# The second MLP matrix with VectorE and ScalarE in source order, and its first G on GpSimd's queue

## The chip, the core and the metric

The kernel runs on one core of one Trainium2 chip. The time is device microseconds (us) of one execution. Five engines work side by side, each through its own list of instructions: TensorE (PE, with PEld for its weight loads), VectorE (DVE), ScalarE (ACT), GpSimd (POOL) and SyncE (SP). DMA transfers are issued from SP's and POOL's lists and move data by themselves.

## The reference

One layer of a diffusion backbone on 512 tokens of width 2048. The part that matters here is the end of the layer, a squared-ReLU MLP with a hidden width of 8192:

```
def sqrelu_mlp(h, w1, w2):
    return jnp.square(jax.nn.relu(h @ w1)) @ w2

x = x + g2 * rms_norm(sqrelu_mlp(modulate(rms_norm(x, norm_g[i, 2]), sh2, sc2), w_mlp_in[i], w_mlp_out[i]), norm_g[i, 3])
```

Everything is float32. Ahead of the MLP stand the modulation vectors, a norm, a Fourier mixing and a projection.

## The kernel before

**Precision.** A float32 operand is split in two: ACT casts it to a rounded high half (`hi`), DVE subtracts that from the operand and gets the low half (`lo`). Three matmuls then make one product (`mm3`, L122): high by low, low by high, high by high. The first of them reads the low half of the weights, so PE can't start a product before that half is there.

**First matrix.** The hidden rows are made in 32 units of 256 (`unit`, `unit_plain`). `unit` is a Strassen-like scheme: seven products A11, S1, S3, S2, A12, A22, S4 of sums of blocks instead of eight, each 24 matmuls with 256 columns. The sums of the left operand are in `comb`. The last unit (31) is a plain one. Each unit's squared Relu G is stored to DRAM (`square_out`, the tensors `gd`).

**Second matrix.** `second(c, j)` is called for seven chunks `c` of 1024 hidden rows and two halves `j` of the output columns: 14 calls of seven products, 24 matmuls of 128x512 each. For a product DVE first adds blocks of the weights (L941, L946, L950, L954; two instructions of 128x1024 each, A11, A12 and S4 need none), then `split` makes `hi` and `lo` of both weight halves (L119 on ACT, L120 on DVE). `hi` and `lo` have three buffers each, a product needs two, so the second half's cast waits until PE has read the first half of the product before. A product's sums are copied out of PSUM by ACT (L928, two copies) when the next product has been traced (`settle`), and POOL adds them to DRAM.

**The left operands** of a chunk come from G: `g_chunk` loads two tiles of 1 MB, `left_in` makes the seven left operands, each with a cast (L902, ACT) and a low half (L903, DVE), four of them with an addition or subtraction on DVE ahead (L891, L894, L897, L900; each 128x1024). The table `NEXT` says behind which product of the chunk before they are traced. Chunk 0's are all made ahead of the first product, at a higher priority. `early` loads two more units of G and splits them for the last part of the kernel.

**What sets the order.** A scheduler with a model of time orders every engine's list; code in `tc.manual_schedule(engines=...)` keeps the order of the source on the engines named, `issue_after(x)` puts instructions behind x on x's engine. Before, all of this stage was left to the scheduler, but for S1 of the first call, which stands behind the cast of S1's left operand. `stream` takes weight buffers in turn, ten in all, and its loads stand on SP's list.

Of the kernel before, what the change touches and what calls it, by code (L numbers as in the profile page):

```python
# [58 lines left out]
def block_kernel(ctx: ExitStack, tc, xs, c_l, w_mod, b_col, g_col,  # L59
# [54 lines left out]
    def as32(ap):  # L114
        return ap.bitcast(F32)
# [533 lines left out]
    def act_relu2(u, srcs):  # L649

        r = tmp4([P, 2, 512])
        for j in range(2):
            nc.scalar.activation(out=r[:, j, :], in_=srcs[j], func=AF.Relu)
        square_out(u, r)
# [120 lines left out]
    def settle():  # L775
        while owed:
            owed.pop(0)()

    def unit(u):

        b11, b12, b22, b21 = (stream(w_in_s[u - UNIT0, b].rearrange("p k f -> p (k f)")) for b in range(4))

        x_, y_ = bank(), bank()
        a_, b_, c_, d_ = x_[:, T0], x_[:, T1], y_[:, T0], y_[:, T1]

        def product(s, src, ps, start):
            wh, wl = hi4([P, 1024]), lo4([P, 1024])
            split(wh, wl, src)
            for k in range(8):
                ks = slice(k * P, (k + 1) * P)  # L790
                lh, ll = left_of(s, k)
                nc.tensor.matmul(ps, lhsT=wh[:, ks], rhs=ll, start=start and k == 0, stop=False, skip_group_check=True)  # L792
                nc.tensor.matmul(ps, lhsT=wl[:, ks], rhs=lh, start=False, stop=False, skip_group_check=True)  # L793
                nc.tensor.matmul(ps, lhsT=wh[:, ks], rhs=lh, start=False, stop=k == 7, skip_group_check=True)  # L794

        product("A11", b11, a_, True)
        flip[0] ^= 1
        both = raw("raw" if flip[0] else "rawm")
        nc.vector.tensor_add(out=both, in0=b11, in1=b12)
        product("S1", both, d_, True)  # L800
        settle()
        sn, r = tmp4([P, 4, 256]), tmp4([P, 1024])
        nc.scalar.copy(out=sn[:, 0], in_=a_)
        nc.vector.tensor_add(out=b12, in0=b12, in1=b22)
        product("S3", b12, c_, False)
        nc.scalar.copy(out=sn[:, 2:4].rearrange("p a t -> p (a t)"), in_=y_)
        nc.vector.tensor_add(out=b11, in0=b12, in1=b11)
        product("S2", b11, b_, False)
        product("A12", b21, a_, False)
        nc.vector.tensor_add(out=b12, in0=b11, in1=b21)  # L810
        product("A22", b12, c_, False)
        nc.vector.tensor_sub(out=sn[:, 1], in0=sn[:, 0], in1=b_)
        nc.vector.tensor_add(out=sn[:, 2], in0=sn[:, 2], in1=sn[:, 3])
        nc.vector.tensor_add(out=r[:, 768:1024], in0=sn[:, 1], in1=sn[:, 2])
        product("S4", b22, d_, False)
        nc.scalar.activation(out=r[:, 0:256], in_=a_, func=AF.Relu)
        nc.scalar.activation(out=r[:, 768:1024], in_=r[:, 768:1024], func=AF.Relu, scale=-1.0)

        def rest():
            nc.vector.tensor_add(out=r[:, 256:768].rearrange("p (a t) -> p a t", a=2), in0=y_.rearrange("p (a t) -> p a t", a=2),  # L820
                                 in1=sn[:, 1].unsqueeze(1).to_broadcast([P, 2, 256]))
            nc.scalar.activation(out=r[:, 256:512], in_=r[:, 256:512], func=AF.Relu)
# [44 lines left out]
    def g4(shape, dt=F32):  # L867
        return buf("g4", shape, dt)
# [1 line left out]
    PRODUCTS = ("A11", "S1", "S3", "S2", "A12", "A22", "S4")  # L870
    pacc = {(s, j): dp.tile([P, 2, 512], F32, name=f"p{s}{j}") for s in PRODUCTS for j in range(2)}
    left = [{} for _ in range(CHUNKS)]
    first_cast = []
    raws = [{} for _ in range(CHUNKS + 1)]

    def g_chunk(c):
        gf = [buf("ga", [P, 4, 512]) for _ in range(2)]
        for j in range(2):
            nc.sync.dma_start(out=gf[j].rearrange("p u t -> p (u t)"), in_=gd[c][:, j].rearrange("p u t -> p (u t)"))
        raws[c]["g"] = gf  # L880

    def left_in(c, s):

        st = raws[c]
        gf = st["g"]
        a11, a21, a12, a22 = gf[0][:, :, T0], gf[0][:, :, T1], gf[1][:, :, T0], gf[1][:, :, T1]
        if s in ("A11", "A12", "A22"):
            src = {"A11": a11, "A12": a12, "A22": a22}[s]
        elif s == "S1":
            src = st["v"] = tmp4([P, 4, 256])  # L890
            nc.vector.tensor_sub(out=src, in0=a22, in1=a21)  # L891
        elif s == "S3":
            src = tmp4([P, 4, 256])
            nc.vector.tensor_sub(out=src, in0=a11, in1=a21)  # L894
        elif s == "S2":
            src = st["v"]
            nc.vector.tensor_add(out=src, in0=src, in1=a11)  # L897
        else:
            src = st["v"]
            nc.vector.tensor_sub(out=src, in0=src, in1=a12)  # L900
        t = buf("ga" if s == "A11" else "s1" if s == "S1" and c % 2 == 0 else "sb", [P, 2, 4, 256], F32R)
        cast = nc.scalar.copy(out=t[:, 0], in_=src)  # L902
        nc.vector.tensor_tensor(out=t[:, 1], in0=src, in1=as32(t[:, 0]), op=ALU.subtract)  # L903
        left[c][s] = t
        return cast

    def second(c, j):

        def load(b):
            return [stream(w_out_s[c, j, b, h].rearrange("p k n -> p (k n)")) for h in range(2)]  # L910

        def product(s, src):
            ps = [bank(), bank()]
            for h in range(2):
                wh, wl = hi4([P, 1024]), lo4([P, 1024])
                split(wh, wl, src[h])
                for k in range(2):
                    ks = slice(k * 512, (k + 1) * 512)
                    for i in range(2):
                        ts = slice(i * P, (i + 1) * P)  # L920
                        t = left[c][s]
                        mm3(ps[i], t[:, 0, 2 * h + k, ts], t[:, 1, 2 * h + k, ts], wh[:, ks], wl[:, ks], h + k == 0, h + k == 2)
            settle()

            def out():
                ev = g4([P, 2, 512])
                for i in range(2):
                    nc.scalar.copy(out=ev[:, i, :], in_=ps[i])  # L928
                if c:
                    nc.gpsimd.dma_start(out=pacc[s, j], in_=ev, accum_op=ALU.add)  # L930
                else:
                    nc.gpsimd.dma_start(out=pacc[s, j], in_=ev)
            owed.append(out)
            for f in THEN.get((c, j, s), ()):
                f()

        b11, b12 = load(0), load(1)
        product("A11", b11)
        both = [g4([P, 1024]) for _ in range(2)]
        for h in range(2):  # L940
            nc.vector.tensor_add(out=both[h], in0=b11[h], in1=b12[h])  # L941
        b22 = load(2)
        with tc.issue_after(first_cast[0]) if c + j == 0 else nullcontext():
            product("S1", both)
        for h in range(2):
            nc.vector.tensor_add(out=b12[h], in0=b12[h], in1=b22[h])  # L946
        product("S3", b12)
        b21 = load(3)
        for h in range(2):
            nc.vector.tensor_add(out=b11[h], in0=b12[h], in1=b11[h])  # L950
        product("S2", b11)
        product("A12", b21)
        for h in range(2):
# [25 lines left out]
            nc.vector.scalar_tensor_tensor(out=oacc[2 + i][:, right_c], in0=u2[:, h], scalar=-1.0, in1=p["S1"][:, h], op0=ALU.mult, op1=ALU.subtract)  # L979


    NEXT = {(0, "A12"): ("A11",), (0, "S4"): ("S1",), (1, "A11"): ("S3",), (1, "A12"): ("S2",), (1, "S4"): ("A12", "A22")}
    THEN = {}
    for c in range(CHUNKS - 1):
        THEN[c, 0, "S3"] = [lambda c=c: g_chunk(c + 1)]
        for (j, s), what in NEXT.items():
            THEN[c, j, s] = [lambda c=c, n=n: left_in(c + 1, n) for n in what]
        THEN[c + 1, 0, "S1"] = [lambda c=c: left_in(c + 1, "S4")]

    gts = {}  # L990

# [10 lines left out]
            g_in(u, lambda: (t[:, 0], t[:, 1]))  # L1002
        oacc.extend(buf("sb" if i else "ga", [P, D]) for i in range(4))

    THEN[CHUNKS - 1, 0, "A12"] = [early]
    with tc.high_priority(offset=AHEAD):
        g_chunk(0)
        for s in PRODUCTS:
            cast = left_in(0, s)
            if s == "S1":  # L1010
                first_cast.append(cast.ins)
            if s == "S3":
                with tc.issue_after(cast.ins):
                    act_relu2(UNITS - 1, last)
    for c in range(CHUNKS):
        for j in range(2):
            second(c, j)
    settle()

    f0, f1 = LAST[0]  # L1020
    for n in (0, 2, 1, 3):
# [150 lines left out]
```

## Time and profile before

| what | value |
|---|---|
| median of 3 runs | 1616.63 us (1615.22 to 1620.12) |
| profiled execution | 1621.48 us, span 1619.7 us |
| PE busy | 1566.8 us, 97% of the span, 9753 matmuls |
| DVE busy | 1251.4 us, 77% |
| ACT busy | 853.6 us, 53% |
| DMA | 365.09 MB, mean 225 GB/s |

The second MLP matrix begins at 964.7 us. Chunk 0 takes until about 1050 us, each further one some 78 us, the last ends near 1520; then come the gathering of the partial sums, the last eight hidden tiles and the final norm. The profile gives each instruction's start and length, and in brackets how long its engine sat idle before it and for whom. The ends of matmuls are modelled: one of 128x512 is shown with 0.39 us, while the next starts 0.23 us after it.

### The profile page before, as it was taken

The numbers are of one execution on the slowest core, as the hardware profiler recorded it, in microseconds if no ns is written. First come the engines' busy times: TensorE is split into PE (matmuls) and PEld (weight loads), VectorE is DVE, ScalarE is ACT, GpSimd is POOL, SyncE is SP. The second block draws the span as 40 slices with busy tenths as digits, with TensorE's granted clock in tenths as the row PEclk, the third lists the DMA queues.
The fourth block names the chain that finished last, engine by engine and source line by source line (L and its number), as shares of the span: only waits on it lengthen the run. The fifth ranks groups of instructions, "written<-read, shape, count | busy, mean of one in ns | idle before, by whom it ended". The sixth has DMA issues, their size and how long they took to land.

```text
span 1619.7 us, 24743 instructions
## 1 busy us (share of the span) xinstructions
PE 1566.8 (97%) x9753; PEld 1329.1 (82%) x9753; DVE 1251.4 (77%) x1545; ACT 853.6 (53%) x1235; POOL 106.2 (7%) x144
## 2 busy tenths in 40 slices
PE   5999998999999999999999989999999999999997
PEld 4766664678899999999999977878878787878886
DVE  7776868675888888888777659979797969767687
ACT  7443336335554545455555537757575757665442
POOL 0000000000000000000000000111111111111100
PEclk9999998999999999999999999999999999999999
DMA  9987889886255555555443456779898988888972
GB/s 380 335 294 291 327 321 358 313 310 250 98 179 187 171 172 177 188 179 185 138 130 135 143 183 245 248 199 252 199 249 215 238 219 198 203 212 199 313 280 104
DMA packets 98325, 365.09 MB, mean 225 GB/s; under 512 B 11109, under 2 KB 11125, under 8 KB 95393
## 3 DMA queue, kind: packets, MB, share of 16 engines
q1 hardware_dynamic: 78992, 294.30, 50.7%
q0 software_dynamic: 19216, 69.22, 19.8%
q8 instruction: 76, 1.25, 0.3%
q14 instruction: 41, 0.33, 0.1%
HBM read 286.92 MB, written 76.55 MB: 224 GB/s over the span
## 4 chain that ended last, share of the span: by engine, by line
PE 79%; DVE 10%; DMA 6%; issue 3%; ACT 2%; DVEq 0%; SPq 0%; ACTq 0%
PE ps L123 16%; PE ps L124 16%; PE ps L125 16%; PE ps L793 9%; PE ps L794 8%; PE ps L792 8%; PE mv L206 3%; DMA raw<-in_w_mod 3%; DVE lo L120 2%; PE mv L172 1%; DVE sb L903 1%; DVE raw L946 1%; DMA ga<-gd 1%; DMA raw<-gd 1%; ACT hi L119 1%
## 5 line engine op out<-in xcount | busy, mean ns | idle before, releaser
L120 DVE TENSOR_TENSOR lo<-raw,hi 128x1024 fp32r<-128x1024 f32 x379 | 461.0, 1222 | 185.8 <-ACT hi L119 183.6
L119 ACT CAST hi<-raw 128x1024 fp32r<-128x1024 f32 x379 | 398.3, 1051 | 316.3 <-PE ps L125 147.1
L123 PE MATMUL ps<-lo,sb 128*128 128x512 f32 x608 | 238.0, 391 | 5.7 <-DVE lo L120 5.6
L124 PE MATMUL ps<-hi,sb 128*128 128x512 f32 x608 | 236.6, 389 | 0.0
L125 PE MATMUL ps<-hi,sb 128*128 128x512 f32 x608 | 236.6, 389 | 0.0
L793 PE MATMUL ps<-big,lo 128*128 128x256 f32 x600 | 170.2, 284 | 0.0
L794 PE MATMUL ps<-big,hi 128*128 128x256 f32 x600 | 169.8, 283 | 0.0
L792 PE MATMUL ps<-big,hi 128*128 128x256 f32 x600 | 169.6, 283 | 0.0
L928 ACT COPY g<-ps 128x512 f32<-128x512 f32 x196 | 114.6, 588 | 91.9 <-PE ps L125 83.8
L123 PEld LDWEIGHTS ps<-lo,sb 128*128 128x128 f32 x608 | 114.1, 188 | 34.0 <-DVE lo L120 10.8
L125 PEld LDWEIGHTS ps<-hi,sb 128*128 128x128 f32 x608 | 114.1, 188 | 23.9
L124 PEld LDWEIGHTS ps<-hi,sb 128*128 128x128 f32 x608 | 114.1, 188 | 23.4
L793 PEld LDWEIGHTS ps<-big,lo 128*128 128x128 f32 x600 | 115.2, 192 | 0.3 <-DVE lo L120 0.2
L794 PEld LDWEIGHTS ps<-big,hi 128*128 128x128 f32 x600 | 115.2, 192 | 0.0
L792 PEld LDWEIGHTS ps<-big,hi 128*128 128x128 f32 x600 | 115.1, 192 | 0.0
L793 PE MATMUL ps<-g,lo 128*128 128x256 f32 x400 | 113.8, 285 | 1.1 <-DVE lo L120 1.0
L792 PE MATMUL ps<-s,hi 128*128 128x256 f32 x400 | 113.2, 283 | 0.0
L794 PE MATMUL ps<-s,hi 128*128 128x256 f32 x400 | 113.2, 283 | 0.0
L793 PE MATMUL ps<-s,lo 128*128 128x256 f32 x400 | 113.2, 283 | 0.0
L794 PE MATMUL ps<-g,hi 128*128 128x256 f32 x400 | 113.0, 283 | 0.0
L792 PE MATMUL ps<-g,hi 128*128 128x256 f32 x400 | 112.3, 283 | 0.0
L221 DVE SCALAR_TENSOR_TENSOR row<-raw,sil,row 128x512 f32<-128x512 f32 x105 | 78.2, 749 | 21.8 <-DMA raw<-in_w_mod 20.8
(291 smaller groups left out, 3279.6 us busy)
## 6 DMA issues: line engine op xcount, KB each, us to landing
raw<-in_w_mod SPq DMA_DIRECT2D x192, 512.0 KB, 5.4
raw<-in_w_out_s SPq DMA_DIRECT2D x112, 512.0 KB, 5.7
raw<-in_w_in_s SPq DMA_DIRECT2D x100, 512.0 KB, 3.9
pS<-g POOLq DMA_DIRECT2D x56, 512.0 KB, 6.3
pA<-g POOLq DMA_DIRECT2D x42, 512.0 KB, 7.0
raw<-in_wf SPq DMA_DIRECT2D x32, 512.0 KB, 5.5
gd<-tmp POOLq DMA_DIRECT2D x32, 512.0 KB, 3.8
ga<-gd SPq DMA_DIRECT2D x14, 1024.0 KB, 6.6
```

The lines of the kernel that those rows point to most:

```text
L119: nc.scalar.copy(out=hi, in_=src)
L120: return nc.vector.tensor_tensor(out=lo, in0=src, in1=as32(hi), op=ALU.subtract)
L123: nc.tensor.matmul(ps, lhsT=ah, rhs=bl, start=start, stop=False)
L124: nc.tensor.matmul(ps, lhsT=al, rhs=bh, start=False, stop=False)
L125: nc.tensor.matmul(ps, lhsT=ah, rhs=bh, start=False, stop=stop)
L172: nc.tensor.matmul(mv[:, 256 + cb:257 + cb], lhsT=rows[:, cb * P:(cb + 1) * P], rhs=ones[:, 0:1], start=True, stop=True)
L206: nc.tensor.matmul(st["ps"][32 * j:32 * j + 32, 0:256], lhsT=cst[:, kq * 4 + j, :], rhs=t[:, j * 256:(j + 1) * 256], start=(kq == 0), stop ...
L221: nc.vector.scalar_tensor_tensor(out=rows, in0=t[:, j * 512:(j + 1) * 512], scalar=sil[:, kt:kt + 1], in1=rows, op0=ALU.mult, op1=ALU.add)
L792: nc.tensor.matmul(ps, lhsT=wh[:, ks], rhs=ll, start=start and k == 0, stop=False, skip_group_check=True)
L793: nc.tensor.matmul(ps, lhsT=wl[:, ks], rhs=lh, start=False, stop=False, skip_group_check=True)
L794: nc.tensor.matmul(ps, lhsT=wh[:, ks], rhs=lh, start=False, stop=k == 7, skip_group_check=True)
L928: nc.scalar.copy(out=ev[:, i, :], in_=ps[i])
```

## The change

In the second matrix DVE and ACT now keep the order of the source, and the source is arranged by products. Chunk 0's left operands but A11 and S1 are traced behind the products of its own first half; `NEXT` gets one table for chunk 0 and one for the others. The first product stands behind S1's left operand (its cast on ACT, its low half on DVE), the last unit's Relu copies behind that cast. Chunk 0's G is loaded on POOL's queue instead of SP's, chunk 1's is traced behind A22 instead of S3. In unit 30 the product S4 is traced, and runs on PE, ahead of A12 and A22.

```diff
         product("S2", b11, b_, False)
+        if u == UNITS - 2:
+            product("S4", b22, d_, False)
         product("A12", b21, a_, False)
...
-        product("S4", b22, d_, False)
+        if u < UNITS - 2:
+            product("S4", b22, d_, False)
...
-            nc.sync.dma_start(out=gf[j].rearrange("p u t -> p (u t)"), in_=gd[c][:, j].rearrange("p u t -> p (u t)"))
+            queue = nc.sync if c else nc.gpsimd
+            queue.dma_start(out=gf[j].rearrange("p u t -> p (u t)"), in_=gd[c][:, j].rearrange("p u t -> p (u t)"))
...
-        product("A11", b11)
-        both = [g4([P, 1024]) for _ in range(2)]
-        for h in range(2):
-            nc.vector.tensor_add(out=both[h], in0=b11[h], in1=b12[h])
+        with ExitStack() as behind:
+            for ins in first_two if c + j == 0 else ():
+                behind.enter_context(tc.issue_after(ins))
+            product("A11", b11)
+            both = [g4([P, 1024]) for _ in range(2)]
+            for h in range(2):
+                nc.vector.tensor_add(out=both[h], in0=b11[h], in1=b12[h])
         b22 = load(2)
-        with tc.issue_after(first_cast[0]) if c + j == 0 else nullcontext():
-            product("S1", both)
+        product("S1", both)
...
-    NEXT = {(0, "A12"): ("A11",), (0, "S4"): ("S1",), (1, "A11"): ("S3",), (1, "A12"): ("S2",), (1, "S4"): ("A12", "A22")}
+    REST = {(1, "S2"): ("S3",), (1, "A22"): ("S2",), (1, "S4"): ("A12", "A22")}
+    NEXT = ({(0, "S4"): ("A11",), (1, "A11"): ("S1",), **REST}, {(0, "A12"): ("A11",), (0, "S4"): ("S1",), **REST})
...
+    for s, what in (("S1", ("S3",)), ("S3", ("S2",)), ("S2", ("A12", "A22")), ("A12", ("S4",))):
+        for w in what:
+            then(0, 0, s, lambda w=w: left_in(0, w))
     for c in range(CHUNKS - 1):
-        THEN[c, 0, "S3"] = [lambda c=c: g_chunk(c + 1)]
...
+        then(c, 0, "S3" if c else "A22", lambda c=c: g_chunk(c + 1))
...
-        for s in PRODUCTS:
-            cast = left_in(0, s)
-            if s == "S1":
-                first_cast.append(cast.ins)
-            if s == "S3":
-                with tc.issue_after(cast.ins):
-                    act_relu2(UNITS - 1, last)
-    for c in range(CHUNKS):
-        for j in range(2):
-            second(c, j)
-    settle()
+        for s in ("A11", "S1"):
+            cast, low = left_in(0, s)
+        first_two += [cast.ins, low.ins]
+        with tc.issue_after(cast.ins):
+            act_relu2(UNITS - 1, last)
+    with tc.manual_schedule(engines={mybir.EngineType.DVE, mybir.EngineType.Activation}):
+        for c in range(CHUNKS):
+            for j in range(2):
+                second(c, j)
+        settle()
```

Three places of the lists follow. In the changed kernel the line numbers are higher (L906, L907 are the left cast and low half, L932 the copies, L948, L952, L956, L960 the additions, L904 the subtraction for S4).

ACT where the second matrix begins, before: `hi_10064` is the second weight half of A11 (the first stands ahead of it), `hi_10090` and `hi_10106` are S1's, L653 the Relu copies of unit 31.

```order
L119 CAST hi_10064<-raw_10040 128x1024
L902 CAST ga_10006<-ga_10002 128x1024
L902 CAST s_1393_10011<-tmp_10009 128x1024
L119 CAST hi_10090<-g_1411_10080 128x1024
L902 CAST sb_10016<-tmp_10014 128x1024
L119 CAST hi_10106<-g_1412_10081 128x1024
L902 CAST sb_10025<-tmp_10009 128x1024
L902 CAST sb_10028<-ga_10003 128x1024
L902 CAST sb_10031<-ga_10003 128x1024
L928 COPY g_1421_10122<-ps_10046 128x512
L653 ACTIVATE tmp_10019<-ps_9853 128x512
L653 ACTIVATE tmp_10019<-ps_9914 128x512
```

The same place now: `hi_10031` and `hi_10047` are A11's weight halves, `hi_10073` and `hi_10089` S1's, `sb_10111` is S3's left operand.

```order
L906 CAST ga_10006<-ga_10002 128x1024
L906 CAST s_1393_10011<-tmp_10009 128x1024
L653 ACTIVATE tmp_10014<-ps_9853 128x512
L653 ACTIVATE tmp_10014<-ps_9914 128x512
L119 CAST hi_10031<-raw_10021 128x1024
L119 CAST hi_10047<-raw_10023 128x1024
L646 ACTIVATE tmp_10014<-tmp_10014 128x1024
L119 CAST hi_10073<-g_1405_10063 128x1024
L119 CAST hi_10089<-g_1406_10064 128x1024
L932 COPY g_1415_10105<-ps_10029 128x512
L932 COPY g_1415_10105<-ps_10030 128x512
L906 CAST sb_10111<-tmp_10109 128x1024
```

The Relu copies moved from behind S1's casts to ahead of A11's, and S3's left cast from ahead of A11's copies to behind them.

DVE in chunk 1, j = 0, from S1's sums to S3, before: `g_1539` and `g_1540` are S1's weights, `lo_10702` and `lo_10718` their low halves, L946 makes S3's weights, L903 and L900 are left operands.

```order
L941 TENSOR_TENSOR g_1539_10691<-raw_10645,raw_10649 128x1024
L941 TENSOR_TENSOR g_1540_10692<-raw_10647,raw_10651 128x1024
L946 TENSOR_TENSOR raw_10649<-raw_10649,raw_10695 128x1024
L903 TENSOR_TENSOR sb_11173<-tmp_10948,sb_11173 128x1024
L946 TENSOR_TENSOR raw_10651<-raw_10651,raw_10697 128x1024
L120 TENSOR_TENSOR lo_10702<-g_1539_10691,hi_10701 128x1024
L950 TENSOR_TENSOR raw_10645<-raw_10649,raw_10645 128x1024
L120 TENSOR_TENSOR lo_10718<-g_1540_10692,hi_10717 128x1024
L900 TENSOR_TENSOR tmp_10948<-tmp_10948,ga_10782 128x1024
L950 TENSOR_TENSOR raw_10647<-raw_10651,raw_10647 128x1024
L120 TENSOR_TENSOR lo_10746<-raw_10649,hi_10745 128x1024
L120 TENSOR_TENSOR lo_10762<-raw_10651,hi_10761 128x1024
```

The same stretch now; `lo_10748` and `lo_10764` are S3's.

```order
L948 TENSOR_TENSOR g_1539_10693<-raw_10647,raw_10651 128x1024
L948 TENSOR_TENSOR g_1540_10694<-raw_10649,raw_10653 128x1024
L120 TENSOR_TENSOR lo_10704<-g_1539_10693,hi_10703 128x1024
L120 TENSOR_TENSOR lo_10720<-g_1540_10694,hi_10719 128x1024
L904 TENSOR_TENSOR tmp_10381<-tmp_10381,ga_10291 128x1024
L907 TENSOR_TENSOR sb_10740<-tmp_10381,sb_10740 128x1024
L952 TENSOR_TENSOR raw_10651<-raw_10651,raw_10697 128x1024
L952 TENSOR_TENSOR raw_10653<-raw_10653,raw_10699 128x1024
L120 TENSOR_TENSOR lo_10748<-raw_10651,hi_10747 128x1024
L120 TENSOR_TENSOR lo_10764<-raw_10653,hi_10763 128x1024
```

S3's additions moved from ahead of S1's low halves to behind S4's left operand, right ahead of S3's own low halves.

ACT in chunk 1, j = 0, from A12's weights (`hi_10831`, `hi_10847`) to A22's (`hi_10874`, `hi_10890`), before: no left cast stands between them.

```order
L119 CAST hi_10831<-raw_10785 128x1024
L119 CAST hi_10847<-raw_10787 128x1024
L928 COPY g_1575_10863<-ps_10791 128x512
L928 COPY g_1575_10863<-ps_10792 128x512
L119 CAST hi_10874<-raw_10649 128x1024
L119 CAST hi_10890<-raw_10651 128x1024
```

The same place now: `hi_10833` and `hi_10849` are A12's, `hi_10876` and `hi_10892` A22's, `ga_10869` is A11's left operand of chunk 2.

```order
L119 CAST hi_10833<-raw_10787 128x1024
L119 CAST hi_10849<-raw_10789 128x1024
L932 COPY g_1575_10865<-ps_10793 128x512
L932 COPY g_1575_10865<-ps_10794 128x512
L906 CAST ga_10869<-ga_10783 128x1024
L119 CAST hi_10876<-raw_10651 128x1024
L119 CAST hi_10892<-raw_10653 128x1024
```

The left cast of the next chunk's A11 now stands between the copies of the product before and A22's casts; on DVE its low half stands ahead of A22's two additions.

## Rows read from the trace of the kernel before

**Rows 1.** The page: chain that ended last, shares by engine.
```profile
PE 79%; DVE 10%; DMA 6%; issue 3%; ACT 2%; DVEq 0%; SPq 0%; ACTq 0%
```
**Rows 2.** Windows: stretch, its length; PE, PEld, DVE, ACT, POOL busy; clock, DMA.
```profile
1134.00:1212.00 78.00, 76.70 (x336) 62.91 (x336) 63.82 (x56) 51.40 (x64) 11.91 (x14) 1.00 0.92 229
...
1368.00:1455.00 87.00, 83.02 (x357) 67.58 (x358) 62.43 (x55) 51.36 (x64) 12.72 (x15) 0.98 0.85 199
```
**Rows 3.** Waits of PE from 964 us on: total us, times, longest.
```profile
PE ps L123 <- DVE lo L120: 11.9, 10, 3.0
PE ps L124 <- DVE ga L903: 4.5, 1, 4.5
```
**Rows 4.** Timeline of PE, first product: start, length, what [idle before].
```profile
964.70 0.61 PE L123 MATMUL ps<-lo,ga 128*128 128x512 f32 x2
969.78 0.80 PE L124 MATMUL ps<-hi,ga 128*128 128x512 f32 x1 [4.46 <-DVE ga L903]
...
972.83 0.39 PE L123 MATMUL ps<-lo,ga 128*128 128x512 f32 x1
```
**Rows 5.** Timeline of ACT and DVE around the start of the second matrix.
```profile
960.42 1.05 ACT L902 CAST ga<-ga 128x1024 fp32r<-128x1024 f32 x1
...
978.84 1.08 ACT L653 ACTIVATE tmp<-ps 128x512 f32<-128x512 f32 x2
...
963.96 2.35 DVE L946 TENSOR_TENSOR raw<-raw,raw 128x1024 f32<-128x1024 f32 x2
...
968.50 1.22 DVE L903 TENSOR_TENSOR ga<-ga,ga 128x1024 fp32r<-128x1024 f32 x1
```
**Rows 6.** Timeline of the DMA issues on POOL and SP.
```profile
946.22 0.68 POOL L647 DMA_DIRECT2D gd<-tmp  x1 [19.48 <-ACT tmp L646]
...
990.13 0.54 POOL L932 DMA_DIRECT2D pS<-g  x1 [5.07 <-ACT g L928]
...
951.48 24.39 SPq L879 DMA_DIRECT2D ga<-gd  x4
```
**Rows 7.** The page, DMA issues: count, KB each, median us to landing.
```profile
ga<-gd SPq DMA_DIRECT2D x14, 1024.0 KB, 6.6
```
**Rows 8.** Timelines of PE, ACT and DVE around one product's start.
```profile
1105.80 0.39 PE L125 MATMUL ps<-hi,sb 128*128 128x512 f32 x1
1106.25 0.50 PE L123 MATMUL ps<-lo,sb 128*128 128x512 f32 x1
...
1105.55 1.27 ACT L928 COPY g<-ps 128x512 f32<-128x512 f32 x2 [0.98 <-PE ps L125]
1106.71 1.06 ACT L119 CAST hi<-raw 128x1024 fp32r<-128x1024 f32 x1
...
1109.31 1.06 ACT L119 CAST hi<-raw 128x1024 fp32r<-128x1024 f32 x1 [0.60 <-PE ps L125]
1110.77 1.06 ACT L902 CAST ga<-ga 128x1024 fp32r<-128x1024 f32 x1 [0.41 <-DVE sb L903]
...
1111.86 1.23 DVE L903 TENSOR_TENSOR ga<-ga,ga 128x1024 fp32r<-128x1024 f32 x1
```
**Rows 9.** Timelines of ACT, DVE and PE at S1 of chunk 2.
```profile
1129.78 1.06 ACT L119 CAST hi<-g 128x1024 fp32r<-128x1024 f32 x1
...
1133.57 1.22 DVE L120 TENSOR_TENSOR lo<-g,hi 128x1024 fp32r<-128x1024 f32 x1
...
1134.84 0.50 PE L123 MATMUL ps<-lo,s 128*128 128x512 f32 x1 [1.09 <-DVE lo L120]
```
**Rows 10.** Timelines of ACT and PE at A11 of chunk 6.
```profile
1438.79 1.06 ACT L119 CAST ga<-raw 128x1024 fp32r<-128x1024 f32 x1 [2.81 <-DMA raw<-gd]
...
1445.61 0.50 PE L123 MATMUL ps<-lo,ga 128*128 128x512 f32 x1 [3.05 <-DVE lo L120]
...
1447.47 0.63 PE L124 MATMUL ps<-hi,ga 128*128 128x512 f32 x1
```
**Rows 11.** Timeline of PE at S3 of chunk 0.
```profile
983.48 0.50 PE L123 MATMUL ps<-lo,sb 128*128 128x512 f32 x1 [1.65 <-DVE lo L120]
```

More of the change, by code (lines that the diff above doesn't have):

```diff
@@ L872, in block_kernel @@
     left = [{} for _ in range(CHUNKS)]
-    first_cast = []
+    first_two = []
     raws = [{} for _ in range(CHUNKS + 1)]
@@ L902, in left_in @@
         cast = nc.scalar.copy(out=t[:, 0], in_=src)
-        nc.vector.tensor_tensor(out=t[:, 1], in0=src, in1=as32(t[:, 0]), op=ALU.subtract)
+        low = nc.vector.tensor_tensor(out=t[:, 1], in0=src, in1=as32(t[:, 0]), op=ALU.subtract)
         left[c][s] = t
-        return cast
+        return cast, low
     def second(c, j):
@@ L979, in gather, with then @@
             nc.vector.scalar_tensor_tensor(out=oacc[2 + i][:, right_c], in0=u2[:, h], scalar=-1.0, in1=p["S1"][:, h], op0=ALU.mult, op1=ALU.subtract)
-    NEXT = {(0, "A12"): ("A11",), (0, "S4"): ("S1",), (1, "A11"): ("S3",), (1, "A12"): ("S2",), (1, "S4"): ("A12", "A22")}
+    REST = {(1, "S2"): ("S3",), (1, "A22"): ("S2",), (1, "S4"): ("A12", "A22")}
+    NEXT = ({(0, "S4"): ("A11",), (1, "A11"): ("S1",), **REST}, {(0, "A12"): ("A11",), (0, "S4"): ("S1",), **REST})
     THEN = {}
-    for c in range(CHUNKS - 1):
-        THEN[c, 0, "S3"] = [lambda c=c: g_chunk(c + 1)]
-        for (j, s), what in NEXT.items():
-            THEN[c, j, s] = [lambda c=c, n=n: left_in(c + 1, n) for n in what]
-        THEN[c + 1, 0, "S1"] = [lambda c=c: left_in(c + 1, "S4")]
+    def then(c, j, s, f):
+        THEN.setdefault((c, j, s), []).append(f)
+    for s, what in (("S1", ("S3",)), ("S3", ("S2",)), ("S2", ("A12", "A22")), ("A12", ("S4",))):
+        for w in what:
+            then(0, 0, s, lambda w=w: left_in(0, w))
+    for c in range(CHUNKS - 1):
+        then(c, 0, "S3" if c else "A22", lambda c=c: g_chunk(c + 1))
+        for (j, s), what in NEXT[min(c, 1)].items():
+            for w in what:
+                then(c, j, s, lambda c=c, w=w: left_in(c + 1, w))
+        then(c + 1, 0, "S1", lambda c=c: left_in(c + 1, "S4"))
     gts = {}
@@ L1003, in early @@
         oacc.extend(buf("sb" if i else "ga", [P, D]) for i in range(4))
-    THEN[CHUNKS - 1, 0, "A12"] = [early]
+    then(CHUNKS - 1, 0, "A12", early)
     with tc.high_priority(offset=AHEAD):
         g_chunk(0)
-        for s in PRODUCTS:
-            cast = left_in(0, s)
-            if s == "S1":
-                first_cast.append(cast.ins)
-            if s == "S3":
-                with tc.issue_after(cast.ins):
-                    act_relu2(UNITS - 1, last)
-    for c in range(CHUNKS):
-        for j in range(2):
-            second(c, j)
-    settle()
+        for s in ("A11", "S1"):
[8 more added lines that the diff above has]
+        settle()
     f0, f1 = LAST[0]
```

## The prediction

> **What bounds the kernel now.** Read first the page's chain: TensorE (PE) makes 79% of it [rows 1], so the time can move only where PE waits or runs at a lower clock. Next the windows by stage: in a usual chunk of the second MLP matrix PE is busy 76.70 of 78 us, in the stretch with the last chunk 83.02 of 87, at a mean clock of 0.98 [rows 2]. Next the waits of PE from 964 us on: ten waits for `lo`, 11.9 us, and one for the left operand, 4.5 us [rows 3]. So 16.4 us of idle is all that an order of VectorE (DVE) and ScalarE (ACT) can win here, with little beside it: after a wait a matmul starts 0.39 us after the last one instead of 0.23, 0.16 for each of eleven (1.8), and after the two longest waits the clock fell to its lower level (1.2 of 2.4 GHz). After the first, the eight starts from 969.78 to 972.83 took 3.05 us for seven steps of 0.227 (1.59), so 1.5 lost [rows 4]; after the one at 1445.61 some matmuls took 0.63 instead of 0.39 again [rows 10], about 0.9. One wait of 0.8 in the tail, which the change doesn't touch, is taken off. What the change can touch is 16.4 - 0.8 + 1.6 + 2.4 = 19.6 us.
>
> Where these waits come from. At the start DVE made six additions (each pair 2.35 us) ahead of the low half of A11's left operand, which ran at 968.50, though ACT had its high half at 960.42 [rows 5]. In chunks 1 to 5 the wait is one per chunk, at S1: the cast of its first weight half was done at 1130.84, but DVE did other work first and made `lo` from 1133.57; PE waited 1.09 [rows 9], 1.25 lost. In chunk 6 ACT sat 2.81 us, and once more, on loads of G that the scheduler had put far ahead [rows 10].
>
> **The change, part by part.** Nothing is computed more or less; VectorE and ScalarE get another order. I follow one product from its start T on PE. It has 24 matmuls of 0.227, 5.44 us. If the next one's first `lo` is there 5.4 us after T, PE doesn't wait.
>
> *What stands in the new order.* In each product's step stand its two casts, the two copies of the product before, then the left operand's cast, then the next product's casts. The copies end only after T: the last matmul of a product started at 1105.80, the next product was due at 1106.03, and after the pair of copies ACT went on at 1106.71, so 0.68 after T [rows 8]. Before, the left casts stood between a product's two weight casts, ahead of the copies, and ACT had time there (the second weight cast waits for a buffer, to 3.06 after T: 1109.31 against 1106.25 [rows 8]); the additions were done one or two products ahead.
>
> *Site with a left cast and two additions (A12 to A22, chunks 1 to 5; this left operand is A11 of the next chunk).* Cast from T+0.68, 1.06 long; its low half follows 0.03 later on DVE (1111.83 to 1111.86 [rows 8]); the next DVE instruction starts 1.14 after it (two take 2.35 [rows 5]); addition 1.22; weight cast 0.03+1.06; `lo` 0.03+1.22; PE 0.05 later. Sum 6.52, against 5.44: PE waits 1.08.
>
> *Site with a subtraction ahead of it (S1 to S3, the left operand S4).* DVE is free at T+0.06 (the `lo` of S1's second half, whose buffer is freed 3.06 after A11's start, cast and made), then 1.22 for the subtraction, 0.03+1.06 cast, 0.03+1.14 low half, 1.22 addition, 1.09 cast, 1.25 `lo`, 0.05: 7.15, a wait of 1.71. So a chunk loses 2.79 where it lost 1.25; five chunks 13.95. Steps without additions behind (S2 and A22 of j = 1, S4 of both) cost nothing: with a subtraction they end at -0.15+1.22+0.03+1.06+0.03+1.14+1.22+0.05 = 4.6; the tightest, the chunk's end with two left casts, at 0.68+1.06+0.03+1.14+1.14+1.22+0.05 = 5.3, so its cover is 0.1.
>
> *Chunk 0.* Its left operands, made before in one rush, now stand with the products: S3 behind S1, S2 behind S3, S4 behind A12, each with additions, and chunk 1's S1 with A11 of j = 1. A product that started late has its second `lo` late too, so the chain begins at T+0.2, +1.0, +0.9 and -0.15: ends 7.3, 8.1, 8.0, 6.9; waits 1.85, 2.66, 2.54, 1.5, together 8.55. Before, 1.65 and a smaller wait stood there [rows 11].
>
> *Start.* A11's weight casts now stand behind the two Relu copies of the last plain unit, and the second reads a bank that PE finishes with its last matmul, at 964.9. Two such copies take 1.08 [rows 5], the second some 0.5; so cast from 965.4, done 966.45, `lo` 967.70, PE 967.75 instead of 964.70 [rows 4]: 3.05. Before, A11's first `lo` was there in time. After an idle of 2.9 us the clock probably falls as it did after 3.05 (+1.5). Start 4.55, where 4.46+0.16+1.5 stood.
>
> *G on GpSimd's queue, S4 earlier in unit 30.* SP issued G at 951.48, behind ten loads of weights; GpSimd is free after unit 30's store at 946.22 [rows 6]. S4's tiles are free two products earlier, and the store is the later of the two. G may land some 5 us earlier, but then the Relu copy sets the start; late it is only from about 962.5 on. I cost it at nothing, from -1.5 (no fall of the clock) to +6.6 (one more landing of such a load [rows 7]). On GpSimd's queue the store of unit 31 and the first partial sums stand behind it, due from 968 on, when G is out. On SP chunk 1's G moves from behind S3 to behind A22; the weights' buffers come free at A22's additions as before, two products (10.9 us) ahead of their use, so no load gets late. The Trainium skill, SBUF — State Buffer, "SBUF: two separate sides", says that a DMA from GpSimd's queue can't write its descriptors while VectorE runs an operation in the mode that takes both ports, and that a queue of SP or ACT avoids it; by that rule the change would lose what it moves, and the sum would be that of the late G below. The trace doesn't bear it out for this work: the issue at 990.13 took 0.54 us [rows 6] in a stage where VectorE is busy 64 of 78 us [rows 2].
>
> *Chunk 6.* S1 to S3 as above, 1.71; the two G casts now stand at A12 with two low halves and two additions: 6.52+1.14 = 7.66, a wait of 2.2; their loads come out some 20 us ahead. Together 3.9, where 3.05, a smaller wait and 0.9 of clock stood.
>
> *Sum.* 4.55 + 8.55 + 13.95 + 3.9 = 30.95. The clock after idles of 2.5 and 2.4 us: it did not fall after 1.65 [rows 11] and fell after 3.05 [rows 10]; so between 0 and 3.0 for the two; I take 1.5, since they lie near the middle. 32.4 - 19.6 = +12.8 us. Against the profiled execution's 1621.48 (its span of 1619.7 and 1.8 around it) that is 1634.3; this execution lies 4.85 above the median of 1616.63, to which the same difference gives 1629.
>
> **Rivals.**
> *The new order hides its steps (faster).* Each `lo` now stands directly behind its addition and cast, so the five waits at S1 and chunk 6's waits go; if the left casts found room ahead of the copies, only the start would be left: 1616.6 - 19.6 + 4.6 = 1602. For it: ACT is busy only 51 of 78 us, DVE 64 [rows 2]. Against it: both run in order, and the chain hangs on one end, the copies after T. It decides at 5.44 us from T to the next `lo`.
> *Half of it (no change).* If the sites with additions cost half (copies sooner, or the additions' second half beside the cast): 4.3 + 7 + 2 + 4.6 = 17.9 against 19.6: 1615, within the 0.3% (4.85 us) below which a measurement of this kernel can't tell a change.
> *G lands late.* If GpSimd's load landed 6.6 us after 962.5, A11's start slips by as much: 1636. Against it: on SP the first tile was there by 960.42 [rows 5], nine us after its issue.
> *The clock falls at every long wait* (three more times instead of one): 1629 + 3 = 1632, and G late on top would pass the range.
> *The change doesn't act:* excluded, since the order of both engines is changed in every chunk.
>
> **How the numbers follow.** Forecast 0.62 (1622 to 1634); fewer waits than now 0.15 (1602 to 1611); half cost, no change 0.14 (1612 to 1621); later start or more clock loss 0.09 (to 1638). Slower by over 0.3%: 0.62 + 0.09 = 0.71; same 0.14; faster 0.15. The range 1611 to 1636 leaves out about 0.12 below and 0.05 above; its reach below comes from the cases of the other sign, the forecast's own is 1622 to 1634.
>
> **What would show it.** Right: PE's waits for `lo` are 17 or so instead of 11, two in each of chunks 1 to 5, at S3 and A22 of j = 0, of about 1.6 and 0.9 idle; none at S1 of j = 0; three of 1.7 to 2.5 in chunk 0; the first matmul of A11 at about 967.8 behind the Relu copies. Left casts start 0.7 us after the product. Wrong: the left casts run before the copies, S3 and A22 follow without a gap, or the waits of PE after 964 us sum to under 16 us.

## The result and the profile after

The changed kernel took 1631.28 us (median of 4 runs, 1628.58 to 1632.39), beside 1617.14 us of the kernel before on the same chip (median of 4): a ratio of 1.0081, 95% interval 1.0067 to 1.0096. It is slower by 14.1 us; the forecast was 1629.0, slower by 12.8. The profiled execution took 1631.86 us with a span of 1630.1, PE busy 1567.6 us as against 1566.8 before: the same work with more idle time between.

PE's waits from 955 us on, total, times and longest, where [rows 3] had 11.9 in ten and 4.5 in one:

```profile
PE ps L123 <- DVE lo L120: 27.0, 19, 2.9
```

Two of the 19 lie in the tail (1.3 us; before one of 0.8), so 17 are the second matrix's. The windows of a usual chunk and of chunk 6 around its two waits, columns as in [rows 2]:

```profile
1136.00:1214.00 78.00, 75.40 (x332) 61.72 (x331) 63.08 (x55) 50.74 (x62) 11.91 (x14) 1.00 0.88 223
...
1459.00:1486.00 27.00, 23.28 (x95) 18.47 (x94) 19.08 (x17) 16.43 (x20) 3.39 (x4) 0.94 0.70 171
```

A usual chunk has PE busy 75.40 of 78 us where [rows 2] had 76.70. The timeline of PE at five places: the start, S2 of chunk 0, S3 and A22 of chunk 2, A22 of chunk 6:

```profile
962.08 0.39 PE L125 MATMUL ps<-big,hi 128*128 128x512 f32 x1
965.35 0.79 PE L123 MATMUL ps<-lo,ga 128*128 128x512 f32 x1 [2.88 <-DVE lo L120]
...
967.65 0.63 PE L125 MATMUL ps<-hi,ga 128*128 128x512 f32 x1
...
987.35 0.50 PE L123 MATMUL ps<-lo,sb 128*128 128x512 f32 x1 [2.42 <-DVE lo L120]
...
988.90 0.63 PE L123 MATMUL ps<-lo,sb 128*128 128x512 f32 x1
...
1141.96 0.39 PE L125 MATMUL ps<-hi,s 128*128 128x512 f32 x1
1143.96 0.50 PE L123 MATMUL ps<-lo,sb 128*128 128x512 f32 x1 [1.62 <-DVE lo L120]
...
1160.21 0.39 PE L125 MATMUL ps<-hi,sb 128*128 128x512 f32 x1
1161.58 0.50 PE L123 MATMUL ps<-lo,sb 128*128 128x512 f32 x1 [0.98 <-DVE lo L120]
...
1480.40 0.79 PE L123 MATMUL ps<-lo,sb 128*128 128x512 f32 x1 [2.11 <-DVE lo L120]
1480.99 0.63 PE L124 MATMUL ps<-hi,sb 128*128 128x512 f32 x1
```

A wait is read from start to start: 1141.96 to 1143.96 is 2.00 us where a step is 0.23, so 1.77 lost. Matmuls shown with 0.63 run at the lower clock (one starts 0.43 after the last). ACT at the start, at S3 and A22 of chunk 2, and at A22 of chunk 0:

```profile
962.51 0.60 ACT L653 ACTIVATE tmp<-ps 128x512 f32<-128x512 f32 x1 [1.95 <-PE ps L125]
963.00 1.98 ACT L119 CAST hi<-raw 128x1024 fp32r<-128x1024 f32 x2
...
994.09 1.28 ACT L932 COPY g<-ps 128x512 f32<-128x512 f32 x2 [1.35 <-PE ps L125]
995.27 1.05 ACT L906 CAST sb<-tmp 128x1024 fp32r<-128x1024 f32 x1
...
1138.08 1.05 ACT L906 CAST sb<-tmp 128x1024 fp32r<-128x1024 f32 x1 [0.54 <-DVE tmp L904]
1141.61 2.20 ACT L119 CAST hi<-raw 128x1024 fp32r<-128x1024 f32 x2 [2.48 <-DVE raw L952]
...
1154.51 1.27 ACT L932 COPY g<-ps 128x512 f32<-128x512 f32 x2 [0.98 <-PE ps L125]
1155.68 1.05 ACT L906 CAST ga<-ga 128x1024 fp32r<-128x1024 f32 x1
1159.21 2.20 ACT L119 CAST hi<-raw 128x1024 fp32r<-128x1024 f32 x2 [2.48 <-DVE raw L960]
```

DVE beside it:

```profile
964.07 2.36 DVE L120 TENSOR_TENSOR lo<-raw,hi 128x1024 fp32r<-128x1024 f32 x2 [2.75 <-ACT hi L119]
...
993.92 1.22 DVE L904 TENSOR_TENSOR tmp<-tmp,ga 128x1024 f32<-128x1024 f32 x1
...
1136.82 1.22 DVE L904 TENSOR_TENSOR tmp<-tmp,ga 128x1024 f32<-128x1024 f32 x1
1139.15 1.23 DVE L907 TENSOR_TENSOR sb<-tmp,sb 128x1024 fp32r<-128x1024 f32 x1 [1.11 <-ACT sb L906]
1140.30 2.35 DVE L952 TENSOR_TENSOR raw<-raw,raw 128x1024 f32<-128x1024 f32 x2
1142.68 2.38 DVE L120 TENSOR_TENSOR lo<-raw,hi 128x1024 fp32r<-128x1024 f32 x2
...
1156.76 1.23 DVE L907 TENSOR_TENSOR ga<-ga,ga 128x1024 fp32r<-128x1024 f32 x1 [1.97 <-ACT ga L906]
1157.90 2.35 DVE L960 TENSOR_TENSOR raw<-raw,raw 128x1024 f32<-128x1024 f32 x2
1160.30 2.37 DVE L120 TENSOR_TENSOR lo<-raw,hi 128x1024 fp32r<-128x1024 f32 x2
```

The two fences read as one chain with the engines taking turns. S3: subtraction 1136.82, left cast 1138.08, low half 1139.15, addition 1140.30, weight cast 1141.61, `lo` 1142.68, PE 1143.96. Each starts as the last ends, and each engine sits idle for the other (1.11 on DVE, 2.48 on ACT). At A22 the chain begins where the copies end, at 1155.68.

### The profile page after: what moved, and what is told of

It reads as the page before. It is cut to its first block, busy times and chain, and to the rows that moved or that the text cites. A ratio compares the mean times of both kernels' runs of the same rounds, so it can differ in the third digit from the quotient of the medians.

```text
span 1630.1 us, 24716 instructions
## 1 busy us (share of the span) xinstructions
PE 1567.6 (96%) x9753; PEld 1329.5 (82%) x9753; DVE 1257.6 (77%) x1545; ACT 857.9 (53%) x1235; POOL 107.3 (7%) x146
## 3 DMA queue, kind: packets, MB, share of 16 engines
q0 software_dynamic: 19504, 71.31, 19.6%
## 4 chain that ended last, share of the span: by engine, by line
PE 79%; DVE 10%; DMA 5%; ACT 4%; issue 3%; SPq 0%; DVEq 0%; ACTq 0%
PE ps L123 16%; PE ps L124 15%; PE ps L125 15%; PE ps L793 9%; PE ps L794 9%; PE ps L792 9%; DVE lo L120 4%; PE mv L206 4%; DMA raw<-in_w_mod 2%; ACT hi L119 2%; DMA raw<-in_w_out 1%; PE mv L172 1%; DMA x<-in_xs 1%; ACT sb L906 1%; DVE raw L952 1%
## 5 line engine op out<-in xcount | busy, mean ns | idle before, releaser
L932 ACT COPY g<-ps 128x512 f32<-128x512 f32 x196 | 113.5, 588 | 77.9 <-PE ps L125 70.3
```

## The experiments

The theory: a product starts late where a left operand's steps and two weight additions have to pass in turn through ACT and DVE between one product's start and the next; a further loss is the start, where A11's casts stand behind a copy of PE's last sums. Each kernel was run beside the kernel before; the ratio is to that one.

| kernel | median us | ratio, 95% interval |
|---|---|---|
| changed kernel | 1631.28 | 1.0081 (1.0067 to 1.0096) |
| side edits alone | 1616.27 | 0.9992 (0.9981 to 1.0003) |
| side edits undone | 1631.55 | 1.0086 (1.0072 to 1.0099) |
| left casts ahead of the copies | 1622.61 | 1.0030 (1.0013 to 1.0047) |
| left operands at steps without sums | 1605.82 | 0.9930 (0.9914 to 0.9947) |
| Relu copies behind the casts | 1626.70 | 1.0056 (1.0040 to 1.0072) |
| both | 1604.46 | 0.9924 (0.9911 to 0.9938) |
| left operands at steps without sums, scheduler's order | 1620.29 | 1.0023 (1.0012 to 1.0033) |
| both and chunk 0 | 1602.39 | 0.9908 (0.9894 to 0.9921) |
| both, chunk 0 and start | 1595.59 | 0.9863 (0.9846 to 0.9879) |

**Side edits alone.** The kernel before, with G's queue and S4's place of the changed one:

```diff
+            queue = nc.sync if c else nc.gpsimd
...
+        if u == UNITS - 2:
+            product("S4", b22, d_, False)
         product("A12", b21, a_, False)
...
```

> The kernel before, with only the two side edits: chunk 0's G on GpSimd's queue and S4 ahead of A12 in unit 30; the scheduler still orders VectorE and ScalarE. Theory (the whole loss of 14 us is the new order of the two engines): the time stays at the kernel before's, 1617 us, between -3 us (G earlier shortens the first wait of 4.5 us) and +2 us. Rival (the load on GpSimd's queue and the move of S4 carry a good part of the loss): 1621 to 1631 us, with G landing late or a wait of TensorE in unit 30 and 31.

The time stayed, and so did the wait of 4.46 us: the low half that PE waits for stands behind six additions on DVE, as in [rows 5]. The timeline of DVE in this run:

```profile
957.79 2.35 DVE L945 TENSOR_TENSOR g<-raw,raw 128x1024 f32<-128x1024 f32 x2
960.06 2.35 DVE L950 TENSOR_TENSOR raw<-raw,raw 128x1024 f32<-128x1024 f32 x2
962.33 2.35 DVE L954 TENSOR_TENSOR raw<-raw,raw 128x1024 f32<-128x1024 f32 x2
964.60 1.22 DVE L907 TENSOR_TENSOR ga<-ga,ga 128x1024 fp32r<-128x1024 f32 x1
```

**Side edits undone.** The changed kernel with G on SP's queue and S4 last in unit 30:

```diff
-            queue = nc.sync if c else nc.gpsimd
+            queue = nc.sync
...
-        if u == UNITS - 2:
-            product("S4", b22, d_, False)
...
```

> The changed kernel with the two side edits undone: chunk 0's G on SP's queue again, S4 behind A22 in unit 30; the order of VectorE and ScalarE stays that of the source. Theory (the order carries the loss): 1631 us as the changed kernel, within 2 us, with the same waits at S3 and A22. Rival (G on GpSimd's queue costs, by a load that lands 10.7 us after its issue instead of 6.6 to 8.0): 1625 to 1629 us, with an earlier start. A third way (SP is too late with G, behind ten loads of weights): A11's left operand is late, 1633 to 1636 us.

1631.55 us: the same as the changed kernel, with the same waits of 1.66 and 0.98 in each chunk. The first is 3.3 instead of 2.9, since G's second tile came into a sum on DVE only here:

```profile
958.85 1.23 DVE L892 TENSOR_TENSOR tmp<-ga,ga 128x1024 f32<-128x1024 f32 x1 [0.80 <-DMA ga<-gd]
```

S1's left cast followed at 960.11, and the Relu copies and A11's weight casts stand behind it on ACT, while PE began its last matmul of unit 31 at 960.72 (959.01 and 962.08 in the changed kernel). So in this run the start hung on G and not on PE's last sums. The fall of the clock behind it cost 2.9 us instead of 1.5, and the one in chunk 6 did not come, so the two profiles come out even in part by chance; the medians agree. On both sides the side edits are worth less than the runs can tell, and the order of the two engines carries the loss.

**Left casts ahead of the copies.** In the step of a product the left operands come before the copies of the product ahead:

```diff
+            for f in THEN.get((c, j, s), ()):
+                f()
             settle()
...
             owed.append(out)
-            for f in THEN.get((c, j, s), ()):
-                f()
```

> The changed kernel, with each left operand's cast and low half put ahead of the two PSUM copies instead of behind them. Theory (at A22 the chain hangs on the copies, which end 0.68 us after the product's start; at S3 it hangs on VectorE's subtraction): the waits at A22 of chunks 1 to 5 (0.98 us each, 1.14 lost) go, the one of 2.1 in chunk 6 shrinks to some 0.5 with its fall of the clock, those at S3 (1.64) stay: 5.7 + 1.7 + 1.7 = 9 us less than the changed kernel, 1622 us, range 1621 to 1626. Rival (the work between a product and the next is too much for the two engines in either order): no change, 1631 us.

1622.61 us, 8.7 less than the changed kernel. At A22 of chunks 1 to 6 no wait is left. ACT and DVE on the way to A22 of chunk 2, then PE at S3:

```profile
1151.06 1.05 ACT L906 CAST ga<-ga 128x1024 fp32r<-128x1024 f32 x1
1152.14 1.27 ACT L934 COPY g<-ps 128x512 f32<-128x512 f32 x2
1154.78 2.22 ACT L119 CAST hi<-raw 128x1024 fp32r<-128x1024 f32 x2 [1.36 <-DVE raw L960]
```

```profile
1152.34 1.22 DVE L907 TENSOR_TENSOR ga<-ga,ga 128x1024 fp32r<-128x1024 f32 x1
1153.47 2.36 DVE L960 TENSOR_TENSOR raw<-raw,raw 128x1024 f32<-128x1024 f32 x2
```

```profile
1141.61 0.50 PE L123 MATMUL ps<-lo,sb 128*128 128x512 f32 x1 [1.31 <-DVE lo L120]
```

The cast runs before the copies, and the low half no longer waits. At S3, where DVE's subtraction comes first, the wait stayed but for 0.3 us (1.6 to 1.3): from the subtraction to PE's start the chain takes 7.15 us as before, but DVE began it 0.25 us ahead of S1's start instead of 0.07 behind. In chunk 0 the wait at A22 grew from 0.98 to 1.94: there too a subtraction comes first, and DVE began it 0.4 us behind A12's start, where it had been 0.67 ahead. So the sum came nearer to the expected 9 us than its terms: the shorter waits at S3 (2.0 in all) and a fall of the clock at S2 of chunk 0 that did not come (1.6) were not in it, and neither was what stands against them, 1.0 more at A22 of chunk 0 and new losses of some 0.25 a chunk.

**Left operands at steps without sums.** Only the places in the source change:

```diff
-    NEXT = ({(0, "S4"): ("A11",), (1, "A11"): ("S1",), **REST}, {(0, "A12"): ("A11",), (0, "S4"): ("S1",), **REST})
+    NEXT = ({(0, "S4"): ("A11",), (1, "A11"): ("S1",), **REST}, {(0, "A22"): ("A11",), (0, "S4"): ("S1",), **REST})
...
-    for s, what in (("S1", ("S3",)), ("S3", ("S2",)), ("S2", ("A12", "A22")), ("A12", ("S4",))):
+    for s, what in (("S1", ("S3",)), ("S3", ("S2",)), ("S2", ("A12", "A22")), ("A22", ("S4",))):
...
-        then(c + 1, 0, "S1", lambda c=c: left_in(c + 1, "S4"))
+        then(c + 1, 0, "S2", lambda c=c: left_in(c + 1, "S4"))
...
-    then(CHUNKS - 1, 0, "A12", early)
+    then(CHUNKS - 1, 0, "A22", early)
```

> The changed kernel, with left operands moved to steps whose next product has no additions: in chunks 1 to 6 S4's from behind S1 to behind S2, and A11's of the next chunk from behind A12 to behind A22; in chunk 0 S4's from behind A12 to behind A22; in chunk 6 the two G casts from behind A12 to behind A22. Theory (a wait stands where a left operand and two additions meet ahead of one product): the ten waits at S3 and A22 of chunks 1 to 5, both of chunk 6 and A22 of chunk 0 go, nothing takes their place: 10.7 + 5.7 + 2.3 + 1.7 (clock) + 1.1 = 21.5 us less than the changed kernel, 1610 us, range 1608 to 1614. Rival (the two engines are simply late in source order, wherever the work stands): the waits move to A12 and S4, 1626 to 1632 us.

1605.82 us: 25.5 less than the changed kernel, below the expected range, and 0.7% faster than the kernel before. Its waits, and a usual chunk's window:

```profile
PE ps L123 <- DVE lo L120: 8.8, 6, 2.9
```

```profile
1134.00:1212.00 78.00, 78.00 (x345) 64.53 (x344) 66.19 (x57) 53.23 (x65) 11.92 (x14) 1.00 0.90 235
```

Of the 19 waits the start, S3, S2 and the second S1 of chunk 0, and two in the tail are left; PE is busy 78 of 78 us. The same work stands on the same engines, so it was not too much for them; it stood ahead of the wrong product. Of the 4 us beyond the expectation some 1.6 come from S2 of chunk 0, where the clock did not fall this time (below), and 1.3 from the matmul behind each wait that is gone, which started 0.34 us after the first instead of 0.23; the rest was not traced.

**Relu copies behind the casts.**

```diff
-        with tc.issue_after(cast.ins):
-            act_relu2(UNITS - 1, last)
+    then(0, 0, "A11", lambda: act_relu2(UNITS - 1, last))
```

> The changed kernel, with the two Relu copies (and the square) of unit 31 put behind the two weight casts of the first product A11 instead of ahead of them. Theory (the first product waits for the second Relu copy, which needs TensorE's last matmul of unit 31): the wait of 2.88 us at the start goes with its fall of the clock, 3.0 + 1.3 = 4.4 us, 1627 us. Rival (the start hangs on G's landing, on GpSimd's queue): A11 starts no earlier, 1631 us.

1626.70 us, 4.6 less than the changed kernel. ACT now makes A11's casts before PE's last sums are done, and PE goes on without a gap:

```profile
957.28 2.00 ACT L119 CAST hi<-raw 128x1024 fp32r<-128x1024 f32 x2
...
961.24 0.60 ACT L653 ACTIVATE tmp<-ps 128x512 f32<-128x512 f32 x1 [1.47 <-PE ps L125]
```

```profile
960.82 0.39 PE L125 MATMUL ps<-big,hi 128*128 128x512 f32 x1
961.04 0.39 PE L123 MATMUL ps<-lo,ga 128*128 128x512 f32 x1
```

**Both edits together.** The two diffs above in one kernel.

> Both edits at once: left operands moved to steps without additions, and unit 31's Relu copies behind A11's weight casts. Theory (the two losses are separate): 1605.8 us of the first alone less the 4.5 us that the second gave by itself, 1601.3 us, range 1600 to 1604. Rival (an earlier start only lengthens the three waits left in chunk 0): 1604 to 1606 us.

1604.46 us: the expectation missed, and the time is the rival's, though the longer waits that it names are the smaller part. The first wait and its fall of the clock went, but S3's wait grew from 1.30 to 1.58, S2's from 2.40 to 2.48, and after S2's the clock fell, as it had not in the kernel without the Relu edit. PE in this run:

```profile
983.51 0.50 PE L123 MATMUL ps<-lo,sb 128*128 128x512 f32 x1 [2.48 <-DVE lo L120]
...
984.59 0.63 PE L124 MATMUL ps<-hi,sb 128*128 128x512 f32 x1
...
987.15 0.63 PE L124 MATMUL ps<-hi,sb 128*128 128x512 f32 x1
```

Eight steps of 0.42 instead of 0.23 cost 1.6 us, the longer waits 0.4: of the 4.5 won at the start 2.2 came through by PE's starts, 1.4 by the medians.

**The scheduler's order.** The kernel with left operands at steps without sums, but ACT and DVE left to the scheduler:

```diff
-    with tc.manual_schedule(engines={mybir.EngineType.DVE, mybir.EngineType.Activation}):
+    with nullcontext():
```

> The kernel with the left operands at steps without additions, but VectorE and ScalarE ordered by the scheduler again instead of by the source. Theory (the gain needs the source's order of the two engines, since the scheduler puts additions of later products ahead of a low half that TensorE waits for): a wait of 1.1 us per chunk at S1 is back, and the long wait at the start, 1612 to 1619 us. Rival (where the left operands stand in the source decides, whoever orders): 1604 to 1608 us.

1620.29 us, just above the expected range. The waits of 1.1 at S1 are back in chunks 1 to 5, with three long ones: 3.33 at the start, 4.23 at S3 of chunk 0 and 4.50 at A11 of chunk 6, where ACT again sat on loads of G (4.19 and 2.35):

```profile
1439.88 1.05 ACT L119 CAST ga<-raw 128x1024 fp32r<-128x1024 f32 x1 [4.19 <-DMA raw<-gd]
1443.29 1.04 ACT L119 CAST ga<-raw 128x1024 fp32r<-128x1024 f32 x1 [2.35 <-DMA raw<-gd]
```

So the source's order is not a loss as such: with the left operands well placed it beats the scheduler by 14.5 us.

**Chunk 0 too.** As with both edits, and S3's left operand made at the start, S2's split in two (`sum_in` is its addition on DVE; what `FIRST` names is called ahead of `settle`, so its cast stands ahead of the copies), chunk 1's A11 and S1 moved:

```diff
-    NEXT = ({(0, "S4"): ("A11",), (1, "A11"): ("S1",), **REST}, {(0, "A22"): ("A11",), (0, "S4"): ("S1",), **REST})
+    NEXT = ({(0, "S4"): ("S1",), **REST, (1, "S2"): ("A11", "S3")}, {(0, "A22"): ("A11",), (0, "S4"): ("S1",), **REST})
...
-    for s, what in (("S1", ("S3",)), ("S3", ("S2",)), ("S2", ("A12", "A22")), ("A22", ("S4",))):
+    then(0, 0, "S1", lambda: sum_in(0))
+    FIRST = {(0, 0, "S3"): lambda: left_in(0, "S2")}
+    for s, what in (("S2", ("A12", "A22")), ("A22", ("S4",))):
...
-        for s in ("A11", "S1"):
+        for s in ("A11", "S1", "S3"):
...
```

> As the kernel with both edits, and chunk 0's three waits taken on: S3's left operand is made at the start, S2's sum behind S1's low halves and its cast ahead of the copies of the product before, and chunk 1's A11 and S1 each get a step without additions. Theory (each wait is a left operand and two additions ahead of one product): the waits at S3 (1.5 lost), S2 (2.6) and S1 of the second half (1.5) go: 1601.3 - 5.5 = 1596 us, range 1595 to 1600. Rival (in chunk 0 VectorE has more to do than TensorE, so the waits only move): 1600 to 1603 us.

1602.39 us: missed, and within the rival's range. The three waits went, but two new ones came, 2.67 at S1 and 2.06 at A12 of the second half (it stands behind S2's step, by which the next expectation names it), each with a fall of the clock. The first by ACT's timeline:

```profile
959.75 1.05 ACT L907 CAST sb<-tmp 128x1024 fp32r<-128x1024 f32 x1
964.91 1.09 ACT L653 ACTIVATE tmp<-ps 128x512 f32<-128x512 f32 x2 [4.12 <-DVE sb L908]
```

The Relu copies need a buffer that S3's left operand held, and DVE made the low half that frees it only behind S1's additions; S1's casts waited behind the Relu copies. A wait for a buffer took the place of a wait for data. The second is two left operands in series behind one set of copies: the subtraction for S3's came on DVE only after the low half of A11's.

**The start too.** A11's first half ahead of G's second tile, then S1's and S3's left operands (`start_lefts`: two sums, two casts, two low halves), A11's second half, the Relu copies; chunk 1's A11 ahead of the copies:

```diff
+                if (c, j, s, h) == (0, 0, "A11", 0):
+                    start_lefts()
...
-    FIRST = {(0, 0, "S3"): lambda: left_in(0, "S2")}
+    FIRST = {(0, 0, "S3"): lambda: left_in(0, "S2"), (0, 1, "A11"): lambda: left_in(1, "A11")}
...
```

> As the kernel before this one, with its two new waits taken away. At the start everything is in one order by hand: A11's first weight half ahead of G, then S1's and S3's left operands, then A11's second half, then the Relu copies (which had waited 4.1 us for the low half of S3's left operand, since that frees their buffer). Chunk 1's A11 is cast ahead of the copies behind A11 of the second half, no longer together with S3's. Theory (the two waits came from these two places): the waits of 2.67 at S1 and 2.06 at S2 of the second half go, each with its fall of the clock: 1602.4 - 2.8 - 1.4 - 2.2 - 1.4 = 1594.6 us, range 1593 to 1598. Rival (VectorE has more to do in chunk 0 than TensorE, so a wait comes back at the next product): 1599 to 1602 us.

1595.59 us, as expected: 35.7 less than the changed kernel and 1.4% faster than the kernel before. Its waits, and chunk 0's window (which had 78.67 of 86 busy in the changed kernel):

```profile
PE ps L123 <- DVE lo L120: 1.1, 2, 0.8
```

```profile
964.00:1050.00 86.00, 85.95 (x379) 70.55 (x378) 77.88 (x68) 60.64 (x74) 9.05 (x16) 1.00 0.65 232
```

Only the two waits in the tail are left. The rival, too much work for DVE in chunk 0, falls: DVE is busy 77.88 of 86 us there and PE never waits.

## Why the prediction was right

The sum came out because its places did. Term by term, in us lost from start to start beyond 0.227 a step, added up over PE's starts:

| term | forecast | measured |
|---|---|---|
| start | 3.05 | 3.04 |
| clock after it | 1.5 | 1.5 |
| chunk 0, S3 | 1.85 | 1.46 |
| chunk 0, S2 | 2.66 | 2.58 |
| chunk 0, A22 | 2.54 | 1.14 |
| chunk 0, S1 of j = 1 | 1.5 | 1.45 |
| S3, chunks 1 to 5 | 5 x 1.71 | 8.96 |
| A22, chunks 1 to 5 | 5 x 1.08 | 5.71 |
| chunk 6, S3 and A22 | 3.9 | 4.05 |
| two falls of the clock | 1.5 | 3.2 |
| sum | 32.4 | 33.1 |

Read in the same way, the waits and falls of the clock that the change replaced had cost 20.2 us in the trace before, where the forecast took off 19.6; so the difference is 12.9 by PE's starts, beside the forecast 12.8.

- *What bounds it.* Right: PE's busy time hardly moved (1566.8 to 1567.6). From unit 31's last matmul on all of PE's steps lost 23.5 us before and 36.7 after: 13.2 more, of which 0.8 in the tail; the medians differ by 14.1. The two profiled executions differ by only 10.4 us, mostly because the one after reached the end of unit 31 some 2.4 us earlier.
- *The chains.* Right in place and size. At S3 DVE was free 0.07 us after S1's start (forecast 0.06), at A22 the copies ended 0.68 after A12's (forecast 0.68), and the links of the chain had their durations. Taking the left operands from these places took the waits away, which shows the mechanism, not only the sum.
- *Waits that go.* Right: none at S1 of j = 0 in chunks 1 to 5, and none for loads of G in chunk 6; the 17 waits stand where they were put.
- *Start.* Right by the Relu experiment: A11's cast came 0.49 after the second Relu copy began. A11's first matmul was at 965.35 instead of 967.8 because of those 2.4 us; measured from PE's last matmul it is the forecast's 3.05.
- *Side edits at nothing.* Right on both sides, by the two experiments on them. G landed in time for the start to hang on the Relu copy; from SP's queue it was the later of the two. The rule of the Trainium skill that I had set against it (SBUF — State Buffer, "SBUF: two separate sides": a DMA on GpSimd's queue can't write its descriptors while VectorE runs in the mode that takes both ports) shows no cost here: 0.9992 with the queue and without the order. VectorE's instructions in this stage are TENSOR_TENSOR throughout, and no run shows whether it was ever in that mode.
- *A22 of chunk 0.* Mis-sized, 2.54 for 1.14. I let its chain begin at T+0.9, since a product that starts late has its second `lo` late. But A12 has no additions and didn't start late, so DVE's subtraction ran from 993.92, 0.67 before A12's start, and the chain began where the copies ended, at 995.27, 0.68 behind it, as at the other A22.
- *Clock.* Mis-sized by 1.7: I priced half of two falls, and both came. The two errors and S3's 0.4 cancel nearly, so the time is closer than its terms; that much is luck.
- *The rivals.* "The new order hides its steps" fell in this kernel; it decides where I put it, at 5.44 us from T to the next `lo`: the experiments reach it by moving left operands, not by new work. "Half of it" fell: the sites with additions cost their full 1.14 and 1.79 us each. Taking the copies out of the chain, by casting ahead of them, cleared A22 but not S3. "G lands late" fell. "The clock falls at every long wait" is what this trace shows: three falls behind the three waits above 2 us.

## What to carry to other kernels

When a source order is fixed by hand, check each step against the time the bottleneck gives it: here 5.44 us for a chain through two engines. Two weight additions, cast and `lo` take 3.4 to 3.8 us of it by themselves (in the kernel with left operands at steps without sums S1 of chunk 2 starts at 1129.69 and the next `lo` is done at 1133.45); with a left operand they took 6.6 and 7.2 us, so that this work belongs ahead of a product that needs no additions. Read the chain from the instruction that begins it (here the copies, tied to the product's start, or the subtraction) and count every change of engine; the share of busy time, 51 and 63 of 78 us, says nothing on it. After a wait is removed, look for the buffer that the moved instruction holds.

## What the runs showed of the hardware

The length of PE's idle alone does not settle in these runs whether the clock falls behind it. At A22 of chunk 6 PE sat idle 2.11 us in the changed kernel, and the clock fell (1480.40 above). With the side edits undone it sat 2.11 us at the same place, and the clock stayed:

```profile
1480.71 0.50 PE L123 MATMUL ps<-lo,sb 128*128 128x512 f32 x1 [2.11 <-DVE lo L120]
1481.05 0.39 PE L124 MATMUL ps<-hi,sb 128*128 128x512 f32 x1
```

It fell after 2.06 in the kernel with chunk 0's edits and after 2.42 and 2.48 at S2 of chunk 0, and stayed after 2.40 there in two kernels with left operands moved and after 2.10 at A22 of chunk 6 in the kernel with the Relu copies behind the casts. From 955 us on every idle from 2.67 up brought it down in these traces, none up to 1.94 did. A fall cost 1.5 to 1.7 us, but 2.9 at the start of the kernel with the side edits undone. What decides in between was not tried; it makes a change of 2 us at one wait hard to price.

G's queue moved it by 1 to 3 us: issued at 944.39 on GpSimd's list, its first tile was cast at 953.08 and its second came into a sum at 957.75; issued from 947.72 on SP's, the same steps came at 955.74 and 958.85. Counted from PE's last matmul of unit 31, which came 1.4 us earlier in that run, it is 2.5 to 4 us.
